# Experts' tokens fetched by row from DRAM and transposed, with the residual added on the way out of PSUM and weights packed by partition

## The chip, the cores and the metric

One NeuronCore of a Trainium2 chip runs the whole kernel in one launch. The metric is the device time of one execution in microseconds (us); the median of three runs is compared. The engines are named TensorE (PE, with PEld for its weight loads), VectorE (DVE), ScalarE (ACT), GpSimd (POOL) and SyncE (SP). DMA transfers are issued from the queues of SyncE, ScalarE and GpSimd and are carried out by 16 DMA engines.

## The reference

```python
# x (1, 512, 1024) float32; 4 groups of 8 experts, two experts of one group per token
h = layer_norm(x, ln_emb_g, ln_emb_b)
proj = h @ w_in                              # windowed attention A, latent attention B
mixed = concat(rms_norm(out_a), rms_norm(out_b)) @ w_out
h = layer_norm(ALPHA * h + mixed, ln_attn_g, ln_attn_b)
# hierarchical mixture of experts
g = argmax(h @ w_group + b_group);  top 2 of (h @ w_expert + b_expert) in group g
for e in range(32):
    hid = silu(h @ w_gate[e]) * (h @ w_up[e])          # 1024 -> 256
    y += combine[:, e] * (hid @ w_down[e])             # 256 -> 1024
out = layer_norm(ALPHA * h + y, ln_ffn_g, ln_ffn_b)
```

Everything is float32; ALPHA is 2 ** 0.25.

## The kernel before

The 512 tokens are four tiles of 128 rows (t = 0 to 3). Embedding norm, projections, attention B and attention A come first. As attention A ends, each tile gets its output projection, the norm `ln_attn` (`norm_gain`, `norm_bias`, or `norm_three`), its transpose (`turn`), the routing logits, and the routing itself (`route`, `weights`, some 20 small VectorE operations a tile). For tiles 2 and 3, `last_two`, the order of all engines is written out by hand.

Routing leaves for each tile `Mb` (which experts), `posm` (the place of the token in its expert's list, from a running count) and `cmb` (token number, weight in two parts). Each expert has room for CAP = 64 tokens, and experts are worked off in 16 pairs, so that a pair fills 128 rows. A loop at the end handles experts with more than 64 tokens; its condition is read from the data.

*Gather.* The normed rows are kept in SBUF in two parts, `h2hi` (rounded) and `h2l` (the rest), made by ScalarE and GpSimd (`part_hi`, `part_lo`). A selection matrix (`select`) with a one for each place is multiplied with both parts (L1094, L1095): 64 matmuls of 256 columns for two pairs. That both gathers and transposes: `xT` comes out with the model dimension on partitions. The first group's gather is `gather0`, before the loop; the others run in `meanwhile`, in the middle of a pair.

*A pair.* `gates`: 16 matmuls for each of the two experts, side by side in the halves of the array (L1143). `gated`: SiLU on ScalarE, product on VectorE, two transposes, copy. `down`: 8 matmuls for each expert (L1169). `scatter`: the weighted results go by indirect DMA from GpSimd's queue to the DRAM table `moe_rows` (`yd`; 2 x 512 rows, first and second expert of a token), which was filled with zeros early in the kernel (L434).

*Weights.* An expert has 3 MB. A ring of 6 slots holds three pairs. SyncE's queue, in written order, loads pair p+3 into the slots of pair p as they come free (`load_gu`, `gu_part`, `fill_dn`). A partition takes 8 consecutive model rows of `w_gate` and `w_up` and 2 of `w_down`. The loads of slots 0 and 1 are cut finer.

*The end.* The last two pairs (ND = 14 and 15) are not scattered. Their results are spread to token order by matmuls with the transposed selection (`pz_part`), into PSUM, on top of the residual ALPHA * h, which `pz_res` puts there by three matmuls with ALPHA times the identity (L1226). `total` adds the rows read back from `moe_rows` and sums; then comes the norm `ln_ffn`.

Of the kernel before, what the change touches and what calls it, by code (L numbers as in the profile page):

```python
# [72 lines left out]
def build(tc, A, out):  # L73
# [10 lines left out]
    yd = nc.dram_tensor("moe_rows", (2 * S, D), F32, kind="Internal").ap()  # L84

# [10 lines left out]
    with top:  # L96
# [251 lines left out]
        zr = cqp.tile([P, 256], F32, name="zr")  # L348
        PO.memset(zr, 0.0)
# [154 lines left out]
        woh_ = m2.tile([P, 4, D], F32R, name="wobh", tag="h2h")  # L504
        woh = [woh_[:, k] for k in range(4)]
# [133 lines left out]
        pieces = {0: (m2, m3), 1: (m4, m4), 2: (m1, m1), 3: (m6, m6)}  # L639


        def src(w, e):
            w = w[0, ds(e, 1)] if not isinstance(e, int) else w[0, e:e + 1]
            return w.rearrange("o (p k) f -> p (o k) f", p=P)

        def load_gu(e, slot, i, eng=SY):

            gus = []
            for tag, j, n in gu_tiles(slot, i):
                gus += gu_part(e, slot, tag, j, n, eng)  # L650
            return gus
# [6 lines left out]
        def gu_part(e, slot, tag, j, n, eng=SY):  # L658
            gu = pieces[slot][0].tile([P, 2, n, FF], F32, name="w_" + tag, tag=tag)
            for k, nm in enumerate(("w_gate", "w_up")):  # L660
                eng.dma_start(out=gu[:, k], in_=src(A[nm], e)[:, j:j + n])
            return [gu[:, :, j] for j in range(n)]

# [3 lines left out]
        def new_dn(slot):  # L667

            if slot < 2:
                return [pieces[slot][1].tile([P, 2, 512], F32, name=f"w_dn{slot}{n}", tag=f"dn{slot}{n}") for n in range(2)]  # L670
            dn = pieces[slot][1].tile([P, 2, D], F32, name=f"w_dn{slot}", tag=f"dn{slot}")
            return [dn, dn[:, :, 0:512], dn[:, :, 512:]]

        def fill_dn(e, dn, eng=SY, n=None):
            if len(dn) == 3:
                eng.dma_start(out=dn.pop(0), in_=src(A["w_down"], e))
                return
            for n in range(2) if n is None else (n,):
                eng.dma_start(out=dn[n], in_=src(A["w_down"], e)[:, :, 512 * n:512 * n + 512])

        def load_dn(e, slot, eng=SY):
            dn = new_dn(slot)
            fill_dn(e, dn, eng)
            return dn
# [52 lines left out]
        def norm_stats(t):  # L737
            if t == 0:
                h2["h"] = m2.tile([P, NT, D], F32R, name="h2hi", tag="h2h")
            tl[t]["mv"], tl[t]["rs"] = ln_stats(z[t], LN_EPS / ALPHA ** 2)  # L740

        def norm_tiles(t):
            d = tl[t]
            if t == NT - 1:
                d["zt"], d["hT"] = [[wk[0].tile([P, 512], F32, name=nm, tag="xT", bufs=8) for _ in range(2)]
                                    for nm in ("zt", "h2T")]
            else:
                d["zt"], d["hT"] = [[x_[:, i] for i in range(2)] for x_ in
                                    [rp_.tile([P, 2, 512], F32, name=nm, bufs=1) for nm in ("zt", "h2T")]]
# [30 lines left out]

        def by_j(a, i):
            return a.rearrange("q (j p) -> q j p", j=8)[:, :, 64 * i:64 * i + 64]

        def strided(a):
            return a.rearrange("q (p j) -> q j p", j=8)

# [734 lines left out]
```

## Time and profile before

| | |
|---|---|
| median of 3 runs | 613.58 us (612.48 to 616.74) |
| profiled execution, its own time | 610.06 us |
| its span, first to last instruction | 608.4 us |
| mean granted TensorE clock | 0.985 |
| DMA traffic | 135.28 MB, mean 222 GB/s |

All times of the trace are in us from the start of the span. A matmul's busy time is modelled and counts its latency, so a TensorE busy all the time need not be at its peak. A DMA share of 1 means that all 16 engines had packets in work. "A <- B" in a wait means that A's engine stood until B was done. The rows themselves stand below.

### The profile page before, as it was taken

Reading aid. Unit: us, or ns where it says so; the run is one execution under the profiler, and the core shown is the slowest. Engines: PE = TensorE matmul, PEld = TensorE weight load, DVE = VectorE, ACT = ScalarE, POOL = GpSimd, SP = SyncE. Lnnn points to the kernel's source line nnn. Section 1 sums busy time; section 2 is a strip of 40 time slices with the busy share of each in tenths; the row PEclk is TensorE's granted clock in tenths of the full one; section 3 lists DMA queues with packets and bytes.
Section 4 is the critical chain, followed back from the end, with each engine's and each line's share of the span. In section 5 each row is a group of like instructions: output and inputs, shape, how many; then the busy total and the mean of one; then the engine's idle time right before and its main releaser. Section 6 shows DMA issues by size and latency. Waiting matters only on the chain. (4 is left out here: it accounts for less than half of the span.)

```text
span 608.4 us, 9184 instructions
## 1 busy us (share of the span) xinstructions
PE 569.2 (94%) x3294; PEld 384.2 (63%) x3295; DVE 318.5 (52%) x871; ACT 204.4 (34%) x434; POOL 126.9 (21%) x152
## 2 busy tenths in 40 slices
PE   2899999999899999999998999999999999999990
PEld 1688998799677777777868365455555555553350
DVE  4955465665786666978898613121212121211277
ACT  2356442454574445758632211111111111110141
POOL 1701122212433332115313000000000000000245
PEclk9999999999899999999998999999999999999996
DMA  8982400321220005960348799999999999999523
GB/s 273 282 277 70 138 1 7 120 79 40 87 70 2 1 1 197 309 265 2 139 166 318 244 313 387 386 349 407 409 397 406 412 390 402 407 394 325 192 91 138
DMA packets 56544, 135.28 MB, mean 222 GB/s; under 512 B 11959, under 2 KB 18999, under 8 KB 53936
## 3 DMA queue, kind: packets, MB, share of 16 engines
q1 hardware_dynamic: 54480, 131.06, 59.3%
q0 software_dynamic: 2016, 3.61, 1.6%
q8 instruction: 27, 0.44, 0.3%
q14 instruction: 21, 0.17, 0.1%
HBM read 124.75 MB, written 13.63 MB: 227 GB/s over the span
## 5 line engine op out<-in xcount | busy, mean ns | idle before, releaser
L1143 PE MATMUL p_gu<-w_gu,xT 128*64 128x512 f32 x512 | 113.4, 594 | 0.0
L1143 PEld LDWEIGHTS p_gu<-w_gu,xT 128*64 128x64 f32 x512 | 36.0, 137 | 69.1 <-issue 65.7
L1185 POOL DMA_INDIRECT moe_rows<-y,idx x14 | 15.0, 1068 | 218.1 <-ACT y L1181 218.1
L1169 PE MATMUL p_y<-w_dn,hidT 128*64 128x512 f32 x256 | 58.4, 598 | 0.5 <-DVE hidT L1155 0.5
L1149 DVE TENSOR_TENSOR hid<-hid,p_gu 128x256 f32<-128x256 f32 x16 | 6.7, 422 | 98.5 <-ACT hid L1148 98.5
L1094 PE MATMUL p_g<-sel,h2hi 128*128 128x256 f32 x224 | 56.6, 293 | 0.0
L1095 PE MATMUL p_g<-sel,h2l 128*128 128x256 f32 x224 | 54.1, 280 | 0.0
L1094 PEld LDWEIGHTS p_g<-sel,h2hi 128*128 128x128 f32 x224 | 42.3, 189 | 11.4 <-issue 11.4
L1095 PEld LDWEIGHTS p_g<-sel,h2l 128*128 128x128 f32 x224 | 42.2, 188 | 0.0
L1148 ACT ACTIVATE hid<-p_gu 128x256 f32<-128x256 f32 x16 | 6.1, 384 | 95.2 <-PE p_gu L1143 88.9
L1169 PEld LDWEIGHTS p_y<-w_dn,hidT 128*64 128x64 f32 x256 | 17.0, 137 | 31.5 <-issue 28.8
L595 PE MATMUL ptr<-cst,pr 128*128 128x128 f32 x208 | 34.7, 280 | 0.0
L557 POOL TENSOR_SCALAR pr<-pr,rc 128x512 f32<-128x512 f32 x16 | 25.0, 1564 | 44.6 <-DVE rc L556 44.6
L597 ACT COPY pT<-ptr 128x512 f32<-128x512 f32 (+2 forms) x48 | 22.3, 476 | 25.2 <-PE ptr L595 23.4
L1183 DVE TENSOR_SCALAR y<-p_y,wsl 128x512 f32<-128x512 f32 x14 | 10.5, 750 | 38.2 <-PE p_y L1169 38.2
L595 PEld LDWEIGHTS ptr<-cst,pr 128*128 128x128 f32 x208 | 24.5, 141 | 7.5 <-issue 4.3
L570 ACT ACTIVATE pr<-pmm,bnm 128x512 f32<-128x512 f32 x32 | 22.0, 689 | 16.5 <-DVE bnm L567 13.8
L1096 ACT COPY xT<-p_g 128x512 f32<-128x512 f32 x14 | 8.2, 585 | 56.1 <-PE p_g L1095 56.1
L1181 ACT ACTIVATE y<-p_y,wsl 128x512 f32<-128x512 f32 x14 | 9.6, 687 | 49.1 <-PE p_y L1169 46.0
L567 DVE TENSOR_REDUCE bnm<-pmm 128x1 f32<-128x512 f32 x32 | 21.8, 686 | 4.5 <-PE pmm L214 4.4
L214 PE MATMUL pmm<-wh,htl 128*128 128x512 f32 (+1 forms) x64 | 24.0, 374 | 0.0
L212 PE MATMUL pmm<-wh,hth 128*128 128x512 f32 (+1 forms) x64 | 23.8, 372 | 0.0
(314 smaller groups left out, 1291.3 us busy)
## 6 DMA issues: line engine op xcount, KB each, us to landing
w_gu<-in_w_gate SPq DMA_DIRECT2D x52, 512.0 KB, 10.1
w_gu<-in_w_up SPq DMA_DIRECT2D x52, 512.0 KB, 10.8
w_dn<-in_w_down SPq DMA_DIRECT2D x20, 1024.0 KB, 12.4
w_dn<-in_w_down SPq DMA_DIRECT2D x24, 512.0 KB, 8.2
wf<-in_w_in SPq DMA_DIRECT2D x12, 512.0 KB, 6.8
w_gu<-in_w_gate SPq DMA_DIRECT2D x24, 256.0 KB, 9.0
w_gu<-in_w_up SPq DMA_DIRECT2D x24, 256.0 KB, 8.0
moe_rows<-zr SPq DMA_DIRECT2D x8, 512.0 KB, 7.0
```

The lines of the kernel that those rows point to most:

```text
L212: PE.matmul(ps, ah, bh, start=first, stop=False)
L214: PE.matmul(ps, al, bh, start=False, stop=last)
L557: eng.tensor_scalar(pr[:, :n], pr[:, :n], rc, None, ALU.mult)
L567: V.tensor_reduce(nm, sp, AX.X, ALU.max, negate=True)
L570: exps.append(SC.activation(pr[:, :S], sp, AF.Exp, bias=nm, accum_out=den).ins)
L595: PE.transpose(pt[:, k * P:(k + 1) * P], pr[:, k * P:(k + 1) * P], ident)
L597: ev(pT[:, :n * P], pt[:, :n * P])
L1094: PE.matmul(pg[:, jj, :n], h2["h"][:, t, P * j:P * j + P], sel[t], start=(t == 0), stop=False)
L1095: PE.matmul(pg[:, jj, :n], h2l[t][:, P * j:P * j + P], sel[t], start=False, stop=(t == NT - 1))
L1143: PE.matmul(pg[64 * i:64 * i + 64], xT[j // 2][:, j % 2, 64 * (2 * q + i):64 * (2 * q + i) + 64], ws[i][0][j], start=(j == 0), stop=(j == 7))
L1169: PE.matmul(py[64 * i:64 * i + 64, :], hT[:, j, 64 * i:64 * i + 64], ws[i][1][n][:, j], start=(j == 0), stop=(j == 1))
L1185: PO.indirect_dma_start(out=yd, out_offset=bass.IndirectOffsetOnAxis(ap=idx[:, :1], axis=0), in_=y, in_offset=None, bounds_check=2 * S - 1 ...
```

## The change: what it does

- The normed rows stay whole, in place of `z`. They are written from ScalarE's queue (`keep`) to a new DRAM table, `norm_rows` (`hd`, 512 rows). `h2hi`, `h2l`, `part_hi`, `part_lo`, `gather0` and `gather` go.
- For each pair, `places_mm` and `places_end` make the row numbers; `fetch` reads the 128 rows by indirect DMA on GpSimd's queue into `xg`, which reuses a `z` tile; places past the end are out of bounds and skipped. `columns` transposes the rows by 8 matmuls with the identity into `xT`, then ScalarE scales `xg` in place by ALPHA (first expert of a token) or 0.
- `leave_rows`: as the down projection leaves PSUM, VectorE adds weight times result to the scaled row, in `xg`; `scatter` writes that to `moe_rows`. For pairs 14 and 15 the scaled rows alone are scattered. So each row of `moe_rows` is written exactly once, the zero fill goes, and so do `pz_res` and its matrices.
- Fetch p+4 is issued behind scatter p, whose tile it takes. Fetches 0 to 3 come before the loop.
- On the host, gate and up of an expert are laid side by side and both weights by partition, so that a partition's share of a load is one contiguous run.
- Slot 4's gate and up weights are loaded with the first ones, into space that held the output projection of B.
- From the loop on, the order of all engines is written by hand (before: TensorE and SyncE).

```diff
+    hd = nc.dram_tensor("norm_rows", (S, D), F32, kind="Internal").ap()
...
-        for i in range(2 * S // P):
-            SY.dma_start(out=yd[i * P:(i + 1) * P, :].rearrange("p (a b) -> p a b", a=4),
-                         in_=zr.unsqueeze(1).to_broadcast([P, 4, 256]))
...
+                gu = pieces[slot][0].tile([P, n, 2 * FF], F32, name="w_" + tag, tag=tag)
+                eng.dma_start(out=gu, in_=src(A["w_gu"], e)[:, j:j + n])
...
+        def keep(t, i):
+            SC.dma_start(out=hd[t * P:(t + 1) * P, hs_(i)], in_=tl[t]["zt"][i])
...
+        def fetch(p, pl):
+            xg = pl["xg"] = hp.tile([P, D], F32, name="xg", tag=f"z{p % NT}")
+            PO.indirect_dma_start(out=xg, out_offset=None, in_=hd, in_offset=bass.IndirectOffsetOnAxis(ap=pl["tok"], axis=0),
+                                  bounds_check=S - 1, oob_is_err=False)
...
         for _ in rb:
             pass
         count(b)
-        gather0(a, (2, 3))
+        weights(a)
+        for t in range(b):
+            sel0_(t)
+        pi0 = psd("places")
+        cms0 = [weights_of(p) for p in range(2)]
+        places_mm(pi0, sel0, cms0, range(b))
         place(b)
         sel0_(b)
...
-        weights(a)
         weights(b)
+        places_mm(pi0, sel0, cms0, [b])
+        pls = places_end(pi0, 2)
+        for p in range(2):
+            fetch(p, pls[p])
         overflow()
...
+        def columns(pl, j2, xT, tag="pmm"):
+            pt = ps.tile([P, 4, P], F32, name="p_x", tag=tag, bufs=2 if tag in ("pmm", "pwo") else 1)
+            for k in range(4):
+                PE.transpose(pt[:, k], pl["xg"][:, P * (4 * j2 + k):P * (4 * j2 + k) + P], ident)
+            (V.tensor_copy if j2 else SC.copy)(xT[:, 4 * j2:4 * j2 + 4], pt)
+            if j2:
+                SC.mul(pl["xg"], pl["xg"], pl["of"])
...
+        def leave_rows(hT, ws, pl):
             def put(sl, py):
-                if sl.start:
-                    SC.mul(y[:, sl], py, wsl)
-                else:
-                    V.tensor_scalar(y[:, sl], py, wsl, None, ALU.mult)
+                y = pl["xg"][:, sl]
+                V.scalar_tensor_tensor(y, py, pl["wsl"], y, ALU.mult, ALU.add)
             down(hT, ws, put)
+            scatter(pl)
...
+        group_sel(1)
+        group(1)
+        group_sel(2)
+        for p in (2, 3):
+            fetch(p, plc[p])
+        xT = new_xT()
+        for j2 in range(2):
+            columns(plc[0], j2, xT)
+        sTs = []
+        for p in range(ND):
+            pg = new_gates()
+            gates(pg, xT, ws[p], 0, 8)
+            load_next(p)
+            nx = new_xT()
+            def meanwhile(i):
+                columns(plc[p + 1], i, nx)
+                if i == 1 and p % 2 == 0 and p // 2 + 2 < NP // 2:
+                    group(p // 2 + 2)
+                if i == 1 and p == ND - 2:
+                    sTs.extend(last_places(k, sels[NP // 2 - 1]) for k in range(2))
+            leave_rows(gated(pg, meanwhile), ws[p], plc[p])
+            load_next_dn(p)
+            if p % 2 == 0 and p // 2 + 3 < NP // 2:
+                group_sel(p // 2 + 3)
+            if p + 4 < NP:
+                fetch(p + 4, plc[p + 4])
+            xT = nx
...
         for n in range(2):
-            pz_part(0, n, 1, last=True)
-            pz_part(1, n, 1, last=True)
-            pz_res(2, n)
+            pz_part(0, n, 1)
+            pz_part(1, n, 1)
...
+    gate, up = [np.asarray(inputs[n])[0].reshape(NE, NK, P, FF) for n in ("w_gate", "w_up")]
+    give("w_gu", np.concatenate([gate, up], axis=3).transpose(0, 2, 1, 3))
+    give("w_dn", np.asarray(inputs["w_down"])[0].reshape(NE, 2, P, 2, 512).transpose(0, 2, 3, 1, 4).reshape(NE, P, 4, 512))
```

## Rows read from the trace of the kernel before

**Rows 1.** The page, busy time (span share) and instructions of each engine.

```profile
PE 569.2 (94%) x3294; PEld 384.2 (63%) x3295; DVE 318.5 (52%) x871; ACT 204.4 (34%) x434; POOL 126.9 (21%) x152
```

**Rows 2.** TensorE's waits, 334 to 575 us: total, times, longest.

```profile
PE p_t L1153 <- DVE hid L1149: 1.1, 1, 1.1
```

**Rows 3.** Windows: length, busy time by engine, granted clock, DMA share, GB/s.

```profile
470.00:485.00 15.00, 15.00 (x88) 7.50 (x86) 2.20 (x4) 1.74 (x4) 0.96 (x1) 1.00 1.02 413
562.00:565.00 3.00, 2.48 (x12) 0.58 (x8) 0.00 (x0) 0.34 (x1) 0.00 (x0) 1.00 0.13 40
```

**Rows 4.** Timeline of TensorE: start, duration, line, operation, tiles, count.

```profile
315.20 0.60 PE L777 MATMUL psd<-cst,zt 128*128 128x128 f32 x4
...
427.66 7.09 PE L1143 MATMUL p_gu<-w_gu,xT 128*64 128x512 f32 x32
...
434.68 0.39 PE L1094 MATMUL p_g<-sel,h2hi 128*128 128x256 f32 x1
...
438.90 3.65 PE L1169 MATMUL p_y<-w_dn,hidT 128*64 128x512 f32 x16
...
519.19 2.37 PE L1143 MATMUL p_gu<-w_gu,xT 128*64 128x512 f32 x10
```

**Rows 5.** Timeline of SyncE's queue: transfers issued, with count.

```profile
336.57 0.33 SPq L661 DMA_DIRECT2D w_gu<-in_w_gate  x1
...
396.39 4.63 SPq L679 DMA_DIRECT2D w_dn<-in_w_down  x4
...
549.56 3.23 SPq L679 DMA_DIRECT2D w_dn<-in_w_down  x4
```

**Rows 6.** Timeline of the end, TensorE and VectorE.

```profile
578.24 3.65 PE L1169 MATMUL p_y<-w_dn,hidT 128*64 128x512 f32 x16
...
583.33 0.68 DVE L1429 CUSTOM_DVE_ANT_0 rows<-pz,rows 128x512 f32<-128x512 f32 x1
...
586.00 0.69 DVE L1429 CUSTOM_DVE_ANT_0 rows<-pz,rows 128x512 f32<-128x512 f32 x1 [1.99 <-PE pz L1231]
```

**Rows 7.** GpSimd's DMA queue and the tile `moe_rows`.

```profile
q0 software_dynamic: 2016, 3.61, 1.6%
...
L1185 POOL DMA_INDIRECT moe_rows<-y,idx x14: 962/966/1237, 348.4 to 558.7; - x14
...
DMA to landing us min/median/max: 3.6/7.4/9.2
```

**Rows 8.** Windows with one run length: 2 KB, 4 KB, 8 KB, 2 KB strided.

```profile
405.00:408.75 3.75, 3.75 (x31) 3.44 (x32) 1.10 (x3) 0.20 (x1) 0.00 (x0) 1.00 1.05 399
411.25:416.25 5.00, 5.00 (x26) 1.67 (x24) 0.00 (x0) 0.69 (x1) 0.96 (x1) 1.00 1.03 391
421.25:425.00 3.75, 3.75 (x27) 2.47 (x27) 0.82 (x2) 0.59 (x1) 0.00 (x0) 1.00 1.01 422
548.00:555.50 7.50, 7.50 (x38) 2.52 (x34) 0.85 (x2) 0.38 (x1) 0.00 (x0) 1.00 0.96 308
```

**Rows 9.** Timeline around the loop's start, VectorE, then TensorE.

```profile
320.07 2.02 DVE L760 SCALAR_TENSOR_TENSOR zt<-zt,ln_rs,lngb 128x512 f32<-128x512 f32 x1
...
322.79 0.75 DVE L760 SCALAR_TENSOR_TENSOR zt<-zt,ln_rs,lngb 128x512 f32<-128x512 f32 x1
...
331.20 0.25 DVE L846 SCALAR_TENSOR_TENSOR Mb<-cst,mf,M 128x32 bf16<-128x32 f32 x1
...
335.22 0.14 DVE L852 TENSOR_SCALAR gn<-gm 128x1 f32<-128x1 f32 x1
...
337.16 0.21 DVE L873 TENSOR_TENSOR cmb<-wc,cmb 128x32 fp32r<-128x32 f32 x1
...
334.61 5.80 PE L1143 MATMUL p_gu<-w_gu,xT 128*64 128x512 f32 x26
```

**Rows 10.** Windows with the granted clock before the loop and in its start.

```profile
320.00:324.00 4.00, 3.80 (x18) 3.53 (x19) 3.83 (x6) 1.78 (x3) 2.19 (x3) 0.57 0.97 401
...
342.00:344.00 2.00, 1.48 (x11) 1.11 (x12) 1.24 (x5) 0.13 (x1) 0.00 (x0) 1.00 0.93 279
```

More of the change, by code (lines that the diff above doesn't have):

```diff
@@ L1228, in pz_part @@
[L1228 removed]
+        def pz_part(t, n, i):
+            if i == 0:
+                tg = tags[t, n]
+                pzs[t, n] = ps.tile([P, 512], F32, name="pz", tag=tg, bufs=1 if tg in ("psd", "pac") else 2)
             sT, y2 = parts[i]
             for k in range(2):
[L1231 to L1233 removed]
@@ new lines, in pz_part, with ring, ring4 @@
+                PE.matmul(pzs[t, n], sT[:, t * P:(t + 1) * P], y2[k][n], start=(i == 0 and k == 0), stop=(i == 1 and k == 1))
+        def ring(slot, part, shape, dt, nm):
+            pl = pieces[slot][1 if part == "dn" else 0]
+            return pl.tile(shape, dt, name=nm, tag=part.replace("gu", f"gu{slot}") if part != "dn" else f"dn{slot}")
+        def ring4(slot, nm):
+            ts = [ring(slot, f"gu{i}", [P, 2, D], F32, f"{nm}{i}") for i in range(2)]
+            return [ts[t // 2][:, t % 2] for t in range(NT)]
@@ new lines, in halves, with weighted, put @@
+        def halves(t):
+            return [[t[k][:, 512 * n:512 * n + 512] for n in range(2)] for k in range(2)]
+        def weighted(p, sT, hT, y2, after=lambda n: None):
+            wsl = plc[p]["wsl"]
+            def put(sl, py):
+                n = sl.start // 512
+                SC.activation(y2[0][n], py, AF.Copy, scale=wsl)
+                V.scalar_tensor_tensor(y2[1][n], py, wsl, f32v(y2[0][n]), ALU.mult, ALU.subtract)
+                after(n)
+            down(hT, ws[p], put)
+            parts.append((sT, y2))
@@ new lines, in build, with group_sel, group @@
+        everything = tc.manual_schedule(engines={V.engine, SC.engine, SY.engine, PE.engine, PO.engine})
+        everything.__enter__()
+        plc = dict(enumerate(pls))
+        sels = {}
+        def group_sel(g):
+            sels[g] = [select_tile(2 * g, t) for t in range(NT)]
+        def group(g):
+            pi = ps.tile([P, 512], F32, name="p_i", tag="psd", bufs=1)
+            places_mm(pi, sels[g], [weights_of(2 * g + u) for u in range(2)], range(NT))
+            for u, pl in enumerate(places_end(pi, 2)):
+                plc[2 * g + u] = pl
@@ L1318, in build @@
+        xTs = [xT, new_xT()]
+        for j2 in range(2):
+            columns(plc[ND + 1], j2, xTs[1])
+        for i in range(2):
+            scatter(plc[ND + i])
+        everything.__exit__(None, None, None)
         free = slots(ND - 1)
```

409 lines of the change are left out of this document (114 added, 295 removed).

## The prediction

> **What bounds it now.** I read the page first: TensorE is busy 94% of the span, no other engine much over half [rows 1]. A busy share is no proof, so next the waits of TensorE's queue and the windows of the expert loop (334 to 575 us). The longest wait in the loop is 1.1 us, on `hid` [rows 2]; but the same windows show the 16 DMA engines at a share of 1.02 and 413 GB/s in mid loop, TensorE at the full granted clock [rows 3]. So two things run at their limit together, and the reader has to see which is ahead. TensorE's own pace: a pair's gates start at 427.66 and, six pairs on, at 519.19 [rows 4], 15.26 us a pair. The weight stream's pace is in SyncE's issues: the four `w_dn` loads that end a pair in slots 0 and 1 start at 396.39 and, nine pairs on, at 549.56 [rows 5], 17.0 us a pair. The stream is slower; TensorE lives on the three pairs that the ring holds when the loop starts at 334.61. The last weights land at 562: from there the DMA share is 0.13 [rows 3]. Then TensorE, still behind, works off what it has: the last down projection starts at 578.24, and the span ends 30.2 us later [rows 6], with VectorE's chain of sums and norms as the last thing.
>
> So a cut of TensorE's work alone is worth the 16 us from 562 to 578 and no more; past that, the stream sets the end.
>
> **The change, part by part.**
>
> *TensorE, per pair.* One pair now: gates 7.02 (427.66 to 434.68), gather plus two transposes of `hid` 4.22 (to 438.90), down 3.65 [rows 4]; with every second pair's places that is the 15.26. The gather's 32 matmuls are what is left of the 4.22 without 0.4 for the transposes: 3.8. They go; in come eight 128-column transposes, two groups of four at 0.60 [rows 4], 1.2. But the gather also covered the way SiLU, product, transpose, copy. Now the first four transposes (0.6) cover part of the 1.1 us that `hid` needs [rows 2], so 0.5 shows, and the second four cover the copy. New pair: 7.0 + 0.6 + 0.5 + 0.4 + 0.6 + 0.1 + 3.6 + 0.5 (half of a places group) = 13.3.
>
> *Bytes, per pair.* Weights are 6.29 MB. A scatter moves 3.61 MB / 14 = 0.26 MB [rows 7]; a fetch takes the same valid rows back, 0.26 MB more. Places past the end are skipped, as the scatter's small packets now are.
>
> *Packing.* Contiguous runs become longer: gate and up of one row lie side by side. In windows where, by the issues, one run length fills the engines: 2 KB runs 399 GB/s, 4 KB 391, 8 KB 422, and 2 KB runs taken out of 4 KB rows (the `w_dn` of slots 0 and 1) 308 [rows 8]. By these, a pair now costs 4.19 MB / 0.391 + 2.10 / 0.422 + 0.26 / 0.41 = 16.3 in slots 2 to 5, and 2.10 / 0.399 + 2.10 / 0.391 + 2.10 / 0.308 + 0.6 = 18.1 in slots 0 and 1: mean 16.9, against 17.0 seen, so the rates hold. After: 6.29 / 0.422 = 14.9 in slots 2 to 5; in slots 0 and 1 two thirds are 4 KB runs, 4.19 / 0.391 + 2.10 / 0.422 = 15.7; mean 15.2; plus 0.52 / 0.41 = 1.3 for scatter and fetch: 16.4 us a pair. What packing wins (1.7), the fetch half eats (0.6). Bounds: 16.15 if all 6.82 MB go at 422; 17.65 if packing brings nothing and the fetch costs its 0.63. I take 16.4, from the rows by run length.
>
> The Trainium skill's page "DMA: Bandwidth & Descriptors", section Bandwidth, puts the HBM side of one core at about 358 GB/s and says that this side binds for loads; by it, run length could not matter. The 422 of this trace disagrees, so its only use is to make me doubt the gain of packing (second rival).
>
> *The start of the loop.* Here the change adds a wait. VectorE now finishes routing tile 3 at 331.45, and 3.2 us later the gates start [rows 9]. Some of that comes earlier: the residual's split on GpSimd goes, beside which a 0.75 us `norm_bias` took 2.02 [rows 9] and small routing operations were slow; I count 3.4 us of such stretching and 1.2 of selections and identity scalings that move or go: 326.8. From there the new chain is serial: weights of tile 2, 2.1 (335.22 to 337.37 is such a block [rows 9]), three selections 1.2, place and selection of tile 3 0.6, weights of tile 3 2.1 (both blocks lay behind the gates' start before), the places matmuls 0.3, seven small VectorE operations at 0.19 each 1.3, the fetch, four transposes 0.6, ScalarE's copy 0.6, handoffs 0.3. The trace shows no gather from DRAM; the nearest row is the scatter on the same queue, issued in 0.97 us and landed 3.6 us at least and 7.4 in the median [rows 7]. The DMA engines are idle when the first fetch goes out, so I take 4.5, nearer the 3.6. Sum 13.6: gates start at 340.4; I take 341.5, since VectorE's copy of the second half of `xT` is queued behind the selections and places of groups 1 and 2, which the manual order puts ahead. Bounds 338 (all at the low end) and 346 (the gates wait for that copy).
>
> *At no cost.* The write of `norm_rows` (eight transfers of 256 KB from ScalarE's queue) lies before the loop, where the engines are not full, and is read only after routing. The zero rows (4 MB, early in the kernel) lie beside TensorE's first chunk; their going is worth 0 to 1 us. Slot 4's early load fills a ring that was full anyway when the loop started. In the loop, fetch p+4 waits on GpSimd's queue for scatter p to land, about 7.4 us; behind it only the next scatter is queued, 16 us later, and the fetched rows are needed three pairs on. ScalarE's scaling of the rows and VectorE's sums out of PSUM fit: the two are busy 1.7 and 2.2 us of 15 [rows 3]. If that cover went, the scaling would add about 1.2 us a pair.
>
> *The end.* The residual's matmuls out of PSUM go (24); four of their eight groups sit behind the last down projection. VectorE, not TensorE, ends the span there: it waits only 2.0 us for them, before its second sum at 586.00 [rows 6]. So 2.0 goes. But now the stream, not TensorE, is last: the gains `gb` and the rows of `moe_rows` queue behind the last `w_dn`. I count `gb` 2 us after the last weights, four shuffles 3.0, then two `y2` operations and a sum of rows, 2.3, and VectorE's first sum, from which the end is 25.1 us away now (583.33 to 608.4 [rows 6]) and 23 then: last landing + 30.3. A spell at half clock in the last pairs, when TensorE waits for weights, adds about 1.5.
>
> **Sum.** Gates start 341.5; first free slot is filled 2.0 us later, as now (336.57 [rows 5]), plus 1 because TensorE starts cold: 344.5. Thirteen pairs x 16.4 = 213: last landing 557.5, against 562. Plus 30.3 + 1.5 = 589.3. That is 19 us less than 608.4. The profiled execution took 610.06 around its span of 608.4, and the median of the three runs, 613.58, is 3.5 above it; I move the median by the same 19: 595.
>
> **Rivals.**
>
> 1. *TensorE's floor.* If the stream is faster than I think, TensorE's own work is next: 341.5 + 1.7 cold + 15 x 13.3 + 9.2 to the last down projection = 552, + 28.2 = 580, median 585. For it: a pair's transfers get fewer, six in place of ten, so engines change over less often. Against: even at 422 for every byte the stream needs 16.15 a pair, so it takes a rate that no window of rows 8 has.
>
> 2. *Packing brings nothing and the fetch costs its bytes.* 13 x 17.65 = 229.5, last landing 574, span 606, median 611: no change. For it: the stream is the bound, and the change adds bytes to it; 2 KB and 4 KB rows differ little. Against: the 422 and the 308. This is also how it goes if the change does not do what it says, that is, if the runs are still cut at the old length.
>
> 3. *The clock falls in every pair (slower).* Dense matmuls of the gather give way to short transposes and waits. The trace has one such spell before the loop: after a stretch of little but small matmuls and a short idle, 320 to 324 ran at a granted 0.57 [rows 10], so about 3.4 us at 1.2 GHz, which costs 1.7. One spell a pair makes 15.0 a pair, and 341.5 + 225 + 11 + 28 = 605.5: still no loss. Two spells make 16.7: 341.5 + 250.5 + 12.6 + 28.2 = 633, median 638. It decides from some 15.3 us a pair. Against it: 342 to 344 holds 0.5 us of idle at 1.00 [rows 10], as mid loop has [rows 3]; once the stream is the bound, a slower TensorE only fills its own waits. The Trainium skill's "TensorE: Matmul & The Clock Gate", section on HAM oscillation, says that waits for DMA between bursts of matmuls send the clock back and that each burst then starts cold. The spell above agrees; that it would happen in each pair no row here shows.
>
> **How the numbers follow.** Forecast (stream-bound with longer runs) 0.60, around 595. Rival 1 0.12, around 585. Rival 2, or a start as late as 346 with a slow fetch, 0.16, around 611. Rival 3 0.12. A measurement of this kernel tells about 1% from no change. Faster by over 1% (under 607.4): 0.72; within: 0.16; slower: 0.12. The range runs from rival 1's 585 less 1 to rival 2's 611 plus 1: 584 to 612, which leaves out rival 3 and little else.
>
> **What would show it.** Loop windows with a DMA share near 1 and over 410 GB/s; SyncE's issues 16.4 us a pair apart; TensorE idle on `w_gu` from about the eighth pair, where three pairs of lead at 3.1 us a pair are used up; the gates' first start near 341.5, with the wait on the fetch ahead of it; last weights near 557; VectorE's sums from there as now. I am wrong if the rows fetched slow the stream more than their bytes, if the first fetch takes 10 us, or if TensorE's clock row shows less than 1.00 in the loop's first half.

## The result: 0.9% slower, and the profile after

| | before | after | forecast |
|---|---|---|---|
| median, 13 runs of each | 612.56 us | 618.20 us | 595 (584 to 612) |
| ratio, 95% interval | | 1.0085 (1.0063 to 1.0107) | |
| profiled execution: span | 608.4 | 617.0 | 589.3 |
| mean granted TensorE clock | 0.985 | 0.939 | |
| first gates / first refill issued | 334.61 / 336.57 | 344.68 / 348.04 | 341.5 / 344.5 |
| last down projection starts | 578.24 | 581.66 | |

The time lies outside the range and on the other side. The page of the changed kernel, busy time first, then two rows of slices (15.4 us each):

```profile
PE 534.0 (87%) x2886; PEld 341.7 (55%) x2887; DVE 328.7 (53%) x870; ACT 204.7 (33%) x428; POOL 132.3 (21%) x161
...
PEclk9799999999999999999985799999998899969975
...
GB/s 293 246 2 78 136 1 18 107 79 39 86 70 1 1 1 242 396 258 36 172 114 295 122 381 421 416 412 420 419 412 409 420 412 385 422 420 330 76 257 136
```

TensorE's busy time fell by 35 us against [rows 1], the stream runs at 409 to 422 GB/s in the loop's slices from 370 to 555 us (one has 385), and the kernel is still slower. So the work went as planned and its order in time did not. The windows, to be set beside [rows 3, 10]:

```profile
334.00:350.00 16.00, 10.30 (x44) 6.06 (x46) 8.45 (x43) 3.02 (x3) 4.53 (x4) 0.58 0.28 78
360.00:455.00 95.00, 92.02 (x459) 37.41 (x456) 31.77 (x85) 14.83 (x21) 15.57 (x15) 1.00 1.02 416
470.00:485.00 15.00, 11.53 (x51) 3.95 (x50) 3.04 (x5) 2.12 (x3) 2.03 (x2) 0.96 1.02 420
552.00:556.00 4.00, 4.00 (x12) 1.15 (x10) 0.00 (x0) 0.00 (x0) 0.00 (x0) 0.53 1.01 415
564.00:568.00 4.00, 2.00 (x9) 0.65 (x10) 1.54 (x3) 1.73 (x3) 0.00 (x0) 1.00 0.73 285
568.00:572.00 4.00, 4.00 (x22) 1.67 (x20) 0.84 (x2) 1.38 (x2) 0.54 (x1) 1.00 0.36 144
```

Three things are to be seen. In 334 to 350 the engines moved 78 GB/s: the stream waited for the loop to start. In 470 to 485 TensorE idles 3.5 of 15 us while the DMA share is 1.02: the stream is the bound, as forecast. From 564 on the share decays, 0.73, then 0.36, before the last weights have landed: some DMA engines are done and others are not, as the landings below show.

The loop's start and its pace, then the end, from the timelines (answers to [rows 4 to 6, 9]):

```profile
323.61 3.43 PE L769 MATMUL psd<-wr,h2T 128*128 128x36 f32 x16
329.45 0.25 DVE L810 SCALAR_TENSOR_TENSOR Mb<-cst,mf,M 128x32 bf16<-128x32 f32 x1
339.20 1.28 POOL L931 DMA_INDIRECT xg<-norm_rows,tok  x1 [18.44 <-DVE pge L847]
342.78 1.97 PE L1066 MATMUL p_x<-cst,xg 128*128 128x128 f32 x8 [1.96 <-DMA xg<-norm_rows,tok]
344.68 8.48 PE L1081 MATMUL p_gu<-w_gu,xT 128*64 128x512 f32 x32
348.04 7.22 SPq L649 DMA_DIRECT2D w_gu<-in_w_gu  x6
355.72 3.65 PE L1101 MATMUL p_y<-w_dn,hidT 128*64 128x512 f32 x16
357.69 2.99 SPq L666 DMA_DIRECT2D w_dn<-in_w_dn  x4
359.21 7.04 PE L1081 MATMUL p_gu<-w_gu,xT 128*64 128x512 f32 x32
448.21 7.72 PE L1081 MATMUL p_gu<-w_gu,xT 128*64 128x512 f32 x32
...
546.18 1.94 PE L1081 MATMUL p_gu<-w_gu,xT 128*64 128x512 f32 x2 [2.35 <-DMA w_gu<-in_w_gu]
551.08 5.52 PE L1081 MATMUL p_gu<-w_gu,xT 128*64 128x512 f32 x13 [2.96 <-DMA w_gu<-in_w_gu]
556.44 3.59 PE L1101 MATMUL p_y<-w_dn,hidT 128*64 128x512 f32 x14
562.02 0.99 POOL L1106 DMA_INDIRECT moe_rows<-xg,idx  x1 [27.18 <-DVE xg L1113]
571.46 0.98 POOL L1106 DMA_INDIRECT moe_rows<-xg,idx  x1 [8.45 <-DMA moe_rows<-xg,idx]
576.55 0.97 POOL L1106 DMA_INDIRECT moe_rows<-xg,idx  x1 [4.11 <-issue]
581.05 1.80 POOL L1274 MEMSET gb<- 128x2048 f32 x1 [3.53 <-DMA moe_rows<-xg,idx]
581.66 3.65 PE L1101 MATMUL p_y<-w_dn,hidT 128*64 128x512 f32 x16
584.36 4.47 SPq L1279 DMA_DIRECT2D rows<-moe_rows  x8
591.43 0.69 DVE L1326 CUSTOM_DVE_ANT_0 rows<-pz,rows 128x512 f32<-128x512 f32 x1 [0.49 <-POOL rows L1286]
```

TensorE does seven pairs from 359.21 to 448.21, 12.7 us a pair. At 546 to 556 it runs gates with waits for `w_gu`, and only then the down projection at 556.44, whose rows scatter 13 carries at 562.02. These gates are half of pair 14's, standing ahead of pair 13's down projection. Behind scatter 13 stand scatters 14 and 15 and then `gb`, 9.4, 5.1 and 4.5 us apart; scatter 14 waits by name for the landing of the scatter before it. Then come the rows of `moe_rows`, and VectorE's first sum at 591.43 (583.33 in [rows 6]).

The packets and landings of the weight transfers, counted from the traces. A pair is 6.29 MB on SyncE's queue, counted from the first refill on. A transfer has 16 landings, one from each engine; "spread" is the time from its first to its last landing, a median over the transfers near that time:

```
                               before after  e3    e5    e7    e10   e11   e12   e13
first refill pair landed       357.6  369.0  368.1 357.3 370.1 366.7 372.5 369.2 369.4
us a pair, the next ten        16.88  16.76  16.74 16.26 15.74 16.97 16.69 16.70 17.18
us a pair, the last 7 of them  16.33  16.67  16.66 15.73 15.79 16.99 16.57 16.60 17.09
spread near 400 us             2.6    5.4    5.5    -    3.5   9.2   3.3   3.7    -
spread near 500 us             4.0   12.6   12.4    -    8.0  12.2   4.9   4.9    -
last weights, first landing    561.1  564.8  565.3 554.7 556.1 565.0 567.5 565.5   -
last weights, last landing     565.1  575.2  576.0 556.1 565.9 575.1 572.8 571.5   -
```

The Trainium skill's page "DMA: Bandwidth & Descriptors", section "Why a DMA increments its semaphore by 16 and not by 1", says that the engines of one transfer finish independently and only the full 16 means that the data has landed. The trace agrees: 16 landings, up to 12.8 us apart, and TensorE waits for the last (a load of `w_gu` lands from 541.4 to 551.0, and the gates that stood waiting start at 551.08).

### The profile page after: what moved, and what is told of

Same layout as the page of the kernel before. It is cut to its first block, busy times and chain, and to the rows that moved or that the text cites. A ratio compares the mean times of both kernels' runs of the same rounds, so it can differ in the third digit from the quotient of the medians.

```text
span 617.0 us, 8276 instructions
## 1 busy us (share of the span) xinstructions
PE 534.0 (87%) x2886; PEld 341.7 (55%) x2887; DVE 328.7 (53%) x870; ACT 204.7 (33%) x428; POOL 132.3 (21%) x161
## 5 line engine op out<-in xcount | busy, mean ns | idle before, releaser
L1081 PE MATMUL p_gu<-w_gu,xT 128*64 128x512 f32 x512 | 129.4, 626 | 16.9 <-DMA w_gu<-in_w_gu 16.9
L1081 PEld LDWEIGHTS p_gu<-w_gu,xT 128*64 128x64 f32 x512 | 41.5, 144 | 99.2 <-issue 73.3
L1113 DVE SCALAR_TENSOR_TENSOR xg<-p_y,wsl,xg 128x512 f32<-128x512 f32 x28 | 21.0, 751 | 40.3 <-PE p_y L1101 40.0
L931 POOL DMA_INDIRECT xg<-norm_rows,tok x16 | 16.7, 1046 | 113.8 <-issue 39.0
L1106 POOL DMA_INDIRECT moe_rows<-xg,idx x16 | 16.5, 1033 | 109.7 <-DVE xg L1113 93.9
L1101 PEld LDWEIGHTS p_y<-w_dn,hidT 128*64 128x64 f32 x256 | 18.2, 137 | 30.8 <-issue 28.3
L215 PE MATMUL pmm<-wl,hth 128*128 128x512 f32 (+1 forms) x64 | 23.8, 372 | 0.0
L615 PE MATMUL pac<-pT,vb 128*64 128x128 f32 x256 | 23.7, 282 | 0.0
L1066 PEld LDWEIGHTS p_x<-cst,xg 128*128 128x128 f32 x128 | 14.8, 146 | 14.2 <-issue 8.1
L1066 PE MATMUL p_x<-cst,xg 128*128 128x128 f32 x128 | 20.6, 289 | 2.0 <-DMA xg<-norm_rows,tok 2.0
L586 ACT ACTIVATE pr<-sm,anm 128x257 f32<-128x257 f32 (+1 forms) x32 | 18.2, 569 | 12.2 <-PE ptr L592 6.1
## 6 DMA issues: line engine op xcount, KB each, us to landing
w_gu<-in_w_gu SPq DMA_DIRECT2D x24, 512.0 KB, 18.2
```

Source lines behind the costliest of these rows:

```text
L215: PE.matmul(ps, ah, bl, start=False, stop=False)
L615: PE.matmul(po[64 * j:64 * j + 64, h0 // 2 * P:h0 // 2 * P + P], vfn(k0 + k, h), pp[j][:, k * P:(k + 1) * P], start=(k == 0), stop=(k == n ...
L1066: PE.transpose(pt[:, k], pl["xg"][:, P * (4 * j2 + k):P * (4 * j2 + k) + P], ident)
L1081: PE.matmul(pg[64 * i:64 * i + 64], xT[:, j, 64 * i:64 * i + 64], ws[i][0][j], start=(j == 0), stop=(j == 7))
L1101: PE.matmul(py[64 * i:64 * i + 64, :], hT[:, j, 64 * i:64 * i + 64], ws[i][1][n][:, j], start=(j == 0), stop=(j == 1))
```

## The experiments

The theory to test: the kernel lost at its end (order of two queues), at its start (a late stream), and in an uneven load of the DMA engines, while the pace came out near the forecast. The rival: the fetch slows the stream by more than its bytes, or packing is worth nothing.

**e1, the down projection first.** Pair 14's gates move, in the written order, into the stretch of the loop, behind pair 13's down projection.

```diff
+        pg14 = new_gates()
+        gates(pg14, xT, ws[ND], 0, 8)
...
-        pg = new_gates()
-        gates(pg, xTs[0], ws[ND], 0, 8)
-        hT = gated(pg)
+        hT = gated(pg14)
```

> Edit: the gates of pair 14 are written behind the down projection of pair 13, so that on TensorE's queue none of them stands in front of it; nothing else. Three theories of where the changed kernel loses its end. A (TensorE's order): half of pair 14's gates stand in front of pair 13's down projection, wait twice for weights (2.35 and 2.96 us) and run at half clock, so that projection starts at 556.0 although its `hidT` is there at 543.9. B (the chain of scatters): the scatters of pairs 13, 14 and 15 go out one after the landing of the other, 562.0, 571.5, 576.6, then `gb` 581, then the rows are read, first VectorE sum 591.4. C (the stream alone): the last weights land at about 567 instead of 557.5 and the end follows from that whatever the order. A expects the down projection of pair 13 at about 545, its scatter near 550, the last down projection at 574 to 576 instead of 581.7, first VectorE sum near 583: 7 to 9 us less. B expects the same scatters earlier, so 8 to 11 us less, with the last down projection unchanged. C expects no change, 0 to 2 us.

1.0011 (0.9982 to 1.0039), median 613.51, span 611.5.

```profile
543.39 3.65 PE L1101 MATMUL p_y<-w_dn,hidT 128*64 128x512 f32 x16
548.65 0.99 POOL L1106 DMA_INDIRECT moe_rows<-xg,idx  x1 [13.29 <-DVE xg L1113]
558.00 0.97 POOL L1106 DMA_INDIRECT moe_rows<-xg,idx  x1 [8.35 <-DMA moe_rows<-xg,idx]
566.71 0.97 POOL L1106 DMA_INDIRECT moe_rows<-xg,idx  x1 [7.74 <-ACT y L1169]
575.51 1.80 POOL L1276 MEMSET gb<- 128x2048 f32 x1 [7.82 <-DMA moe_rows<-xg,idx]
```

Down 13 starts 13 us earlier and its scatter follows, but the three scatters and `gb` still queue one behind the other, 8.7 to 9.4 us apart, so VectorE's first sum (586.92) gains only 4.5, less than the 7 to 11 that theories A and B gave.

**e2, the last scatters ahead.** Scatters 14 and 15 go out right behind scatter 12, before their rows are scaled; this kernel leaves that scaling out of the result.

```diff
+            if p == ND - 2:
+                for i in range(2):
+                    scatter(plc[ND + i])
...
-        for i in range(2):
-            scatter(plc[ND + i])
```

> Edit: the rows of pairs 14 and 15 are scattered right behind scatter 12, before they are scaled, so only scatter 13 is left for the end; TensorE's order stays that of the changed kernel. The residual of those pairs' tokens is left unscaled, so the output differs from the reference there; the work is the same. A (TensorE's order): the last down projection stays at 581.7, so the first VectorE sum comes no earlier than 586.8 (5.1 us behind it, as in the kernel before): 4 to 5 us less. B (the chain of scatters is the only limit): scatter 13 at 562, landed by 571, rows read from 571 to 580, first sum near 582: 9 us less. C (the stream alone): no change, 0 to 2 us.

1.0001 (0.9982 to 1.0021), median 612.68, span 611.9.

```profile
574.05 1.80 POOL L1274 MEMSET gb<- 128x2048 f32 x1 [9.22 <-DMA w_dn<-in_w_dn]
583.53 3.65 PE L1101 MATMUL p_y<-w_dn,hidT 128*64 128x512 f32 x16
```

`gb` is ready 7 us earlier, and now TensorE is late: its last down projection starts at 583.53. Each repair alone uncovers the other half.

**e3, both**, with the columns of pairs 14 and 15 and their scaled scatters in the middle of pair 13, so that the whole reference is computed.

```diff
+                if p == ND - 1:
+                    if i == 0:
+                        xTs.extend((nx, new_xT()))
+                    for j2 in range(2):
+                        columns(plc[p + 1 + i], j2, xTs[i])
+                    scatter(plc[p + 1 + i])
+                    return
```

> Edit: both: pair 15's rows are transposed and scaled inside pair 13, the scatters of pairs 14 and 15 go out ahead of scatter 13, and pair 14's gates stand behind pair 13's down projection. A and B together: last down projection near 574, first VectorE sum near 580, 11 to 13 us less than the changed kernel, so about 605 to 607, some 1% faster than the kernel before. C (the stream alone): 0 to 2 us less.

0.9979 (0.9958 to 1.0000), median 610.67; its profiled execution, with a span of 606.2, took 607.82.

```profile
550.37 8.78 PE L1081 MATMUL p_gu<-w_gu,xT 128*64 128x512 f32 x30 [2.90 <-DMA w_gu<-in_w_gu]
576.46 3.65 PE L1101 MATMUL p_y<-w_dn,hidT 128*64 128x512 f32 x16
```

Against the kernel before, that is 6.5 us better than the change (of 612.5), less than the 11 to 13 expected: TensorE still waits for pair 14's weights, until 550.37, and has 26 us of work from there to its last down projection. The last weights land at 576.0 and the span ends 30.2 later, which is the forecast's own 30.3, though put together otherwise: `gb` is filled at 570.29, before the last landing, and VectorE's first sum (581.55) comes 5.1 behind the last down projection, as in [rows 6]. So agreement to 0.1 is partly luck; the other kernels with these two queues in order need 30.5 (e7), 31.2 (e8) and 32.2 (e12). What is left of the loss lies before the last landing.

**e4, the row numbers first.** VectorE's small operations before the loop are split, so that the row numbers of the fetch come before the weights, and the transposes of pair 0 are written ahead of the selections and places of groups 1 and 2.

```diff
+        numbers(b)
+        sel0_(a)
...
+        rows_mm(pr0, sel0, range(b))
...
+        rows_mm(pr0, sel0, [b])
...
+        rows_end(pd0, 2, lambda hs, i: pr0[hs, i:4:2])
+        pls = views(pd0, 2)
+        for p in range(2):
+            fetch(p, pls[p])
         weights(a)
...
+        weights(b)
```

> Edit: for the first two pairs the row numbers are made by eight matmuls of their own as soon as tile 3 is placed, and the fetches go out ahead of the combine weights of tiles 2 and 3; the transposes of pair 0 stand ahead of the selections of groups 1 and 2. The order at the end stays that of the changed kernel. Stream theory (whoever starts the ring's refill sets all landings behind it): first fetch at about 333.5 instead of 339.2, gates at about 339 instead of 344.7, last landing and end 5 to 6 us earlier. Rival (the start is hidden, because from the eighth pair on TensorE waits for weights anyway and the end hangs on the order there): 0 to 2 us.

1.0161 (1.0119 to 1.0202), median 621.82, span 620.4: the edit missed its aim.

```profile
334.18 0.16 DVE L931 TENSOR_TENSOR tok<-idf,of 128x2 int32<-128x2 f32 x1
338.36 1.28 POOL L958 DMA_INDIRECT xg<-norm_rows,tok  x1 [16.99 <-DVE cmb L841]
345.80 0.27 PE L848 MATMUL psd<-Mb,onesb 128*128 128x32 bf16 x4 [1.64 <-DVE pis L946]
348.50 3.72 PE L1116 MATMUL p_gu<-w_gu,xT 128*64 128x512 f32 x10
```

The row numbers are there at 334.34, but the fetch goes at 338.36: it waits for the table. Tile 3's rows go into `norm_rows` by transfers issued at 324.8 and 325.2, among 5.2 MB of prefetched weights, and their last packet ends at about 336.9. The profile puts this wait down to a VectorE operation that the fetch does not need; e8, where the rows are written earlier, bears out the table. Moreover the gates start at 348.50, though VectorE's copy of `xT` ends at 344.66: ahead of them on TensorE's queue stand the overflow's count and the places of group 1, which now wait for VectorE's weights and selections. It tells something all the same: a start 3.8 later makes the first refill pair land 3.6 later (372.6) and the span 3.4 longer. Here the start passes on to the end.

**e8, the start, on e3.** As e4, and tile 3's rows are written from SyncE's queue ahead of the last three `w_dn`, both copies of the first `xT` are ScalarE's, and groups 1 and 2 of the routing move into pairs 0 and 1.

```diff
+            return (SY if t == NT - 1 else SC).dma_start(out=hd[t * P:(t + 1) * P, hs_(i)], in_=tl[t]["zt"][i])
...
+            (V.tensor_copy if j2 and pl is not pls[0] else SC.copy)(xT[:, 4 * j2:4 * j2 + 4], pt)
...
+                if i == 1 and p == 0:
+                    group(1)
+                    group_sel(2)
+                    for k in (2, 3):
+                        fetch(k, plc[k])
```

> Edit: the experiment with both, and a mended start: row numbers of pairs 0 and 1 made ahead of the combine weights; gates of pair 0 no longer behind the places of group 1 and the selections of groups 1 and 2, which move into pair 0; the rows of tile 3 are written to `norm_rows` from SyncE's queue ahead of the last three prefetched `w_dn`. The last point comes from the run with rows first: there the row numbers were ready at 334.3 but the first fetch went out at 338.4, and the write of tile 3's rows, issued at 325.2 among 5.2 MB of weights, is what it still needed. Theory (write of `norm_rows` is on the path, and the start passes on to the end): first fetch at about 334.7, gates at about 341 instead of 344.2, end 3 to 4 us earlier than with both, ratio to the kernel before about 0.992. Rival (the fetch waits for something else): first fetch still near 338.4, gates at 344 or later, no gain.

0.9935 (0.9903 to 0.9968), median 608.82: 2.7 us better than e3 relative to the kernel before, the two intervals just overlapping.

```profile
335.65 1.29 POOL L958 DMA_INDIRECT xg<-norm_rows,tok  x1 [13.62 <-DVE dn L834]
341.96 5.33 PE L1116 MATMUL p_gu<-w_gu,xT 128*64 128x512 f32 x16
345.59 2.04 SPq L649 DMA_DIRECT2D w_gu<-in_w_gu  x2
```

The last packet of tile 3's rows now ends at 331.5, and the fetch goes 0.9 us behind its row numbers (334.76): the table held it in e4. The gates start 2.7 earlier than in the changed kernel, the refill 2.5 earlier. But the first refill pair has landed at 368.0, as in e3 (368.1), and the last weights at 575.9 (576.0 in e3): in these two executions the earlier start does not reach the end. The fetches of pairs 2 and 3 now run beside the first refill (355.70 and 356.99, in e3 342.48 and 343.78); that they use up what was won was not tried. The gain over e3 thus stands on the times alone.

**e7, no refetch, on e3.** Fetches of pairs 4 to 15 are left out.

```diff
-                fetch(p + 4, plc[p + 4])
+                plc[p + 4]["xg"] = plc[p]["xg"]
```

> Edit: the experiment with both (scatters ahead, down projection first), without the 12 fetches of the loop: pairs 4 to 15 work on the tile that pair p-4 left, so their output is not the reference's; transposes, scaling and scatters stay. Bytes theory (the fetch costs the 0.26 MB of its rows at some 415 GB/s, 0.63 us a pair): weights 12 x 0.63 = 7.5 us earlier at the end, the whole kernel 5 to 7 us faster than the one with both, near 604 us. Rival 1 (uneven DMA engines: fetched and scattered rows lie on the first places of each expert, so that a few of the 16 engines carry them and finish late): the same 7.5 us, and the slow fall of the DMA share at the end of the stream (0.73, 0.36, 0.25 in three stretches of 4 us from 564 in the changed kernel) gets steeper too, 10 us or more. Rival 2 (TensorE sets the pace): under 2 us.

0.9768 (0.9713 to 0.9823), median 597.88, span 596.4. The stream needs 15.74 us a pair in place of 16.74: a fetch costs 1.0, where its bytes at the stream's rate are 0.63. Over the last seven pairs it is 0.87. The spread of the landings falls too (8.0 in place of 12.4 near 500 us).

**e5, packing alone.** The kernel before with weights packed by partition.

```diff
-            return w.rearrange("o (p k) f -> p (o k) f", p=P)
+            return w.rearrange("o p a b -> p (o a) b")
...
-            for k, nm in enumerate(("w_gate", "w_up")):
-                eng.dma_start(out=gu[:, k], in_=src(A[nm], e)[:, j:j + n])
+            eng.dma_start(out=gu, in_=src(A["w_gu"], e)[:, j:j + n])
```

> Edit: the kernel before with the weights packed by partition as in the change, and nothing else of it. Forecast's theory (longer runs are worth 1.2 to 1.7 us a pair): the last weights land 15 us or more before 562, TensorE's own 15.26 us a pair becomes the bound, last down projection at 334.6 + 15 x 15.26 + 9.2 = 572.7 instead of 578.2: 5 to 6 us less, ratio about 0.991, no more, because TensorE sets the end. Rival (packing is worth nothing, the stream stays at 16.9 us a pair): no change, ratio 1.00.

0.9997 (0.9971 to 1.0022), median 611.04. A stream at 16.26 us a pair in place of 16.88, and no gain in time:

```profile
364.00:552.00 188.00, 187.68 (x1062) 98.33 (x1060) 43.13 (x159) 20.98 (x38) 11.78 (x11) 1.00 1.00 402
552.00:556.00 4.00, 4.00 (x20) 1.52 (x20) 0.82 (x2) 0.00 (x0) 0.00 (x0) 1.00 0.72 295
556.00:560.00 4.00, 4.00 (x20) 1.29 (x18) 0.36 (x1) 0.69 (x1) 0.96 (x1) 1.00 0.04 14
...
577.86 3.65 PE L1168 MATMUL p_y<-w_dn,hidT 128*64 128x512 f32 x16
```

The weights are in by 556, nine us earlier than before, and TensorE, without a gap from 364 on, starts its last down projection where it did (578.24 in [rows 6]). In the kernel before, TensorE sets the end.

**e10 and e11, dealing the rows out, on the changed kernel.** An expert has 64 places and fewer tokens, and the valid ones are its first. Counting from the data, with places dealt to the 16 engines in fours, one engine gets 112 rows of the 14 pairs' transfers and another 5. Both kernels put the valid places elsewhere: e10 by eights (91 to 21), e11 so that each four has valid places (52 to 57). The diff is e11's.

```diff
+        spread = rl_.tile([P, 4, CAP], F32, name="spread")
+        for u in range(4):
+            for a_ in range(16):
+                k0 = 15 - a_ if u % 2 else a_
+                PO.tensor_copy(spread[:, u, 4 * a_:4 * a_ + 4], iota1[:, k0:CAP:16])
...
-            V.tensor_tensor(sl, pos.unsqueeze(2).to_broadcast([P, n, CAP]),
-                            iota1.unsqueeze(1).to_broadcast([P, n, CAP]), ALU.is_equal)
+            V.tensor_tensor(sl, pos.unsqueeze(2).to_broadcast([P, n, CAP]), spread[:, :n], ALU.is_equal)
```

> Edit: the changed kernel with one constant permuted: the token with number 8b + a in an expert's list takes place 8a + b of 64 instead of place 8b + a, so the places that hold tokens (32 of 64 on average) are spread over the partitions instead of filling the first ones; bytes and instructions are the same. Theory (uneven DMA engines): if the rows of a transfer are dealt to the engines by blocks of partitions, the engines of the first places carried nearly all fetched and scattered rows; in the changed kernel the DMA share falls slowly at the stream's end (1.00, 0.73, 0.36, 0.25 in stretches of 4 us from 560), in the kernel before at once (1.03, 0.59, 0.02 from 556). Then with spread places the fall is steep, the last weights land near 567, TensorE's waits for weights after 455 shrink, and the end is 5 to 9 us earlier than in the changed kernel. Rival (the slow fall is the last transfers' own): within 1 us of the changed kernel.

> Edit: the changed kernel with the places permuted: the first expert's token k of a pair takes place 4 (k mod 16) + k div 16 of its 64, the second expert's 4 (15 - k mod 16) + k div 16. Bytes and instructions of the loop stay; 64 small copies on GpSimd early on make the constant. What it comes from: the trace has 16 landings for each transfer. In the changed kernel the time from first to last of them grows from 1.4 us (361) over 5.3 (406) to 11 (449) and stays there; in the kernel before it reaches 5. With spread places it grew faster (8.5 at 404), and the landings of an indirect transfer fell into 8 early and 8 late ones. That fits rows dealt to 16 engines in fours, place p to engine (p div 4) mod 16: the first places of both experts are the same engines' (112 rows against 5 over 14 pairs by this data's counts); spread places served every second engine (91 against 21); the new order gives each 52 to 57. Theory (engines loaded unevenly by the indirect rows): the 16 landings of a weight transfer stay within 2 or 3 us, the last weights land near 566 instead of 575, TensorE's 8 waits for `w_gu` (16.9 us) shrink by half or more, the end comes 7 to 10 us earlier, ratio 0.993 to 0.998. Rival (the spread of the landings is not from the rows): as with spread places, within 1 us of the changed kernel.

e10: 1.0116 (1.0066 to 1.0167), no gain; its 16 landings come in two bunches of eight, and the spread is no smaller. That is what fours, and not eights, would do. e11: 1.0056 (1.0030 to 1.0083), median 616.26: 1.8 us less than the changed kernel, where 7 to 10 were expected, and the two intervals overlap. The spread near 500 us falls from 12.6 to 4.9, and the share of the DMA engines holds until the end:

```profile
564.00:568.00 4.00, 2.52 (x8) 1.02 (x10) 0.84 (x2) 0.38 (x1) 0.00 (x0) 0.79 0.99 399
568.00:572.00 4.00, 4.00 (x18) 1.53 (x16) 0.75 (x1) 1.37 (x2) 0.97 (x1) 0.79 0.75 300
```

0.99 and 0.75 where the changed kernel had 0.73 and 0.36. The last weights land 2.4 earlier although this execution's gates started 3.3 later (347.96). TensorE's waits for `w_gu` were to halve and did not (14.8 us in all, in place of 16.9), so the spread does not set them.

**e12, e3 with the start of e8 and the dealing of e11.**

> Edit: the mended start with scatters ahead and the down projection first, and the places dealt over the engines. Theory (engines loaded unevenly by the indirect rows): on top of the mended start's 0.9935 another 6 to 9 us, about 600 us, ratio 0.978 to 0.984; TensorE's last down projection near 568. Rival (spread not from the rows): ratio 0.993 again.

0.9871 (0.9834 to 0.9908), median 604.79, span 603.7: faster than both kernels, 7.9 us less than the kernel before and, by the two ratios, 13 less than the changed one. Against e8 the dealing alone is worth 3.9 us here; the two intervals overlap by a hair (0.9903 to 0.9908). TensorE's last down projection starts 1.5 us behind the last landing (571.5), where it was 13.1 in the kernel before:

```profile
572.98 3.65 PE L1141 MATMUL p_y<-w_dn,hidT 128*64 128x512 f32 x16
```

**e13, e12 with the weights laid out as before.** They then meet other model rows, so the result is not the reference's; the work is the same.

```diff
-                eng.dma_start(out=gu, in_=src(A["w_gu"], e)[:, j:j + n])
+                for k, nm in enumerate(("w_gate", "w_up")):
+                    eng.dma_start(out=gu[:, k], in_=src(A[nm], e)[:, j:j + n])
...
-            dn = pieces[slot][1].tile([P, 4, 512], F32, name=f"w_dn{slot}", tag=f"dn{slot}")
-            eng.dma_start(out=dn, in_=src(A["w_dn"], e))
+            dn = pieces[slot][1].tile([P, 2, D], F32, name=f"w_dn{slot}", tag=f"dn{slot}")
+            eng.dma_start(out=dn, in_=src(A["w_down"], e))
```

> Edit: the kernel with all mends, but with the weights laid out and loaded as in the kernel before (2, 4 and 8 KB runs, gate and up apart, ten transfers a pair in place of six); the weights then meet other model rows, so the output is not the reference's, with the same work. Forecast's price of packing: 1.2 to 1.7 us a pair, 16 to 22 us over 13 pairs, if the stream is the bound: 616 to 622 us. Price by the kernel before with packed weights (its stream ended some 9 us earlier, 0.7 us a pair): 9 us more, near 609. Rival (TensorE is the bound in the mended kernel): under 3 us.

0.9939 (0.9911 to 0.9968), median 609.36, 4.2 us slower than e12 relative to the kernel before. The stream needs 17.18 us a pair in place of 16.70, so packing is worth 0.48 here and 0.62 in e5 (0.49 and 0.60 over the last seven pairs).

## Why the prediction was wrong

The bound was named rightly (the stream, once TensorE's gather is gone), and the mechanisms of the loop are there: share over 1, 416 GB/s, TensorE idle on `w_gu` from about 463 (its tenth pair, where the eighth was forecast). The span is 617.0 and not 589.3, 27.7 us more. By the forecast's own terms:

| term of the sum | forecast | measured | us |
|---|---|---|---|
| first free slot filled | 344.5 | 348.04 | 3.5 |
| first refill pair | 16.4 | 21.0 (348.04 to 369.0) | 4.6 |
| twelve more pairs | 12 x 16.4 | 12 x 16.76, to 570.1 | 4.3 |
| last landing, beyond that pace | 0 | 575.2 | 5.1 |
| last landing to the end | 30.3 + 1.5 | 41.8 | 10.0 |

Together 27.5; the rest is rounding of 13 x 16.4.

*The end, 10.0.* "Last landing + 30.3" took the order of the queues for granted. Shown by e1, e2 and e3: half of pair 14's gates stand ahead of down 13 on TensorE's queue, and three scatters to one table go one after the other. The forecast listed the scatters only in the loop, "behind it only the next scatter is queued, 16 us later"; at the end there are three at once, and from the first to `gb` they take 19 us (562.02 to 581.05). With both mended 30.3 comes out within 2 us (e3 30.2, e7 30.5, e8 31.2, e12 32.2), though its parts are others, as said at e3.

*The stream, 14.0 without its start.* "So the rates hold" was said of a pace, not of an end. The sum was never put through the kernel before, which gives 336.57 + 13 x 17.0 = 557.6 where its last weights land from 561.1 to 565.1. The forecast for the change was 557.5. Like for like the sum promised the stream no gain at all, and set against the measured 562 it looked like 4.5. The first refill pair takes 21.0 us in both kernels (336.57 to 357.6; 348.04 to 369.0), which alone is 4.6 of it. The trace shows why: its loads go out only as TensorE works off pair 0, the last four `w_dn` from 357.69 on, behind the down projection that frees their space (355.72), and the stream runs at 311 GB/s in 350 to 365.

*Packing and fetch.* Forecast 1.7 won and 0.63 lost a pair. Measured over the last seven pairs of the table: 0.49 (e13 against e12) to 0.60 (the kernel before against e5) won, and 0.87 lost (e3 against e7). That closes: 16.33 + 0.87 less 0.49 to 0.60 makes 16.60 to 16.71, and the changed kernel has 16.67. So once the loop is under way the change makes the stream slower, by 0.34 us a pair. The better mean of ten pairs, 16.76 against 16.88, comes from the first three (17.0 against 18.2), where in the kernel before SyncE's queue still stops for the landings of scatters and for TensorE:

```profile
SPq L661 <- DMA moe_rows<-y,idx: 16.6, 5, 5.3
395.00:410.00 15.00, 15.00 (x88) 8.06 (x86) 4.44 (x21) 1.66 (x3) 1.20 (x1) 1.00 0.97 344
```

The step that failed is the pricing of a run length by windows of 4 to 8 us; that the mix of transfers in such windows is not steady is the likely reason, not a shown one. The check that "the rates hold", 16.9 against 17.0 seen, took the pace of the issues, which holds such stops too; over the last seven pairs 16.33 landed, so that agreement was luck. Rival 2 (packing nothing, the fetch its bytes: last landing 574, span 606) came nearest in its numbers: 575.2 here, 606.2 in e3. It still was not the mechanism: packing brings something, the fetch costs more than its bytes, and the start, the first refill pair and the last landing bring 13.2 of the 17.7 us by which the weights were late. Why a fetch costs 0.87 to 1.0 and not 0.63 stays open; the smaller spread in e7 speaks for the uneven engines, but e12, with a spread of 4.9, still needs 16.70 a pair.

*The engines, 5.1.* The forecast has no such term. That a fetch has its valid rows in few of the 16 shares is argued from the counts and borne out by e10 (eights: no better) and e11 (fours: spread 4.9, last landing 2.4 earlier). Reckoned as in the table of terms, the last landing comes 5.1 us beyond the pace in the changed kernel, 7.0 in e3 and 4.8 in e10, but 0.1 in e11 and 1.9 in e12. The kernel before has 4.9 too, with its last landings only 4.0 apart; why is open. So the term was missing from the forecast of both, and against the kernel before it costs nothing.

*The start, 3.5.* "The write of `norm_rows` ... at no cost" holds only because the row numbers are late: e4 shows the fetch held for 4 us by that write among prefetched weights, once they come earlier. In the changed kernel itself tile 3's `Mb` is done at 329.70, not 326.8, and the chain to the gates is 15.0, not 13.6, at a clock of 0.58. The forecast prices a cold start for the gates (1 us), none for the routing ahead of them: TensorE, with the gather gone, is busy only 6.1 of 14 us from 320 on (12.4 before) and runs at the lower clock, 1.2 GHz, from 323.6 to 347.5, so that the logits of tile 3 take 3.43 us (323.61) where the kernel before needs 1.96. The fetch took 3.6 from issue to transposes, not 4.5. All in all the loop starts 10 us later than before, and the stream 11.5; e4 shows such a delay paid nearly in full (3.8 us of delay, 3.4 of span).

*Right.* TensorE's pace, 12.7 against 13.3. The clock (rival 3): 1.00 from 360 to 455; half clock only at the loop's start and in three spells from 467 on (467, 484, 546), each at a wait for weights. TensorE's floor (rival 1) never showed, as no stream was fast enough.

So where did the gain go? In the kernel before 43.3 us lie between the last landing and the end (565.1 to 608.4), because TensorE's last down projection starts 13.1 behind that landing. With both queues in order 30.2 to 32.2 are left (e3, e7, e8, e12): that gain is real. The changed kernel got 1.5 of it (41.8), since the order at its end costs some 10, and its weights land 10 us later, for the start's 11.5 less 12 x 0.12 of better pace.

## What to carry to other kernels

Put the model of the stream through the kernel before, from its first issue to its last landing, before it is used on the change; a pace that agrees hides a start and an end that do not. When a bound moves to the weight stream, whatever starts the stream late can pass on to the end nearly in full (e4), so a new serial step ahead of it has to be set against the whole gain. And read the order of each queue at the end of a kernel: an instruction written later can stand earlier, and indirect transfers into one table waited for each other here.

## What the runs showed of the hardware

- Weight transfers beside indirect transfers whose valid rows lie together landed in 16 parts up to 12.8 us apart near 500 us (12.6 in the median); with the rows dealt out by fours it was 4.9 (e11), by eights 12.2 (e10).
- Packing a partition's share of a load from runs of 2 and 4 KB into one run was worth 0.5 to 0.6 us for 6.29 MB (e13, e5).
- Writing 0.5 MB of rows among 5.2 MB of queued weight loads took 12 us from issue to the last packet (e4).
- Indirect transfers to one DRAM table, each waiting for the landing of the one before, went 8.7 to 9.4 us apart while weights streamed, and 4.5 to 5.1 once the engines were nearly idle.
